# One decoder block on one core: two side chains that step at the ends of units, a transpose with a unit of its own, zeros in four parts

## The chip, the core and the metric

The kernel runs on one core of one Trainium2 chip. The metric is the device time of one execution, in microseconds (us). TensorE (PE) multiplies, VectorE (DVE), ScalarE (ACT) and GpSimd (POOL) work element by element, and SyncE (SP) issues most DMAs. Each engine takes its own instructions in the order in which the program wrote them.

## The reference

One layer of a hybrid decoder on x of 4096 tokens by 1024 features, all in float32:

- h = rms_norm(x), times one matrix w_in, whose columns feed two groups of four heads each.
- Group A, gated delta net: a short convolution and SiLU on q, k and v; normalised q and k; per chunk a triangular solve; a state S that is carried from chunk to chunk; a gated norm.
- Group B, retention: rotary phase on q and k; attention inside a chunk with a fixed decay; a state carried from chunk to chunk; a norm, gated by a SiLU gate.
- x = x + [o_a, o_b] w_out. Then a router picks one of 8 groups of experts and two of its 8 experts for each token; each expert is a SwiGLU of 1024 to 256 to 1024; their weighted sum is added to x, and a last norm closes the block.

## The kernel before, in words

**Stages.** The tokens are worked in 8 super-blocks of 512, counted from 0. Each has four stages of some 60 us, in the order (a,1), (b,1), (a,0), (b,0): the letter is the head group, the digit the pair of heads. After the eighth super-block come the output projection and the router, and from about 2568 us on the experts.

**Units.** A stage is a row of units: the projection of one tile (`proj_n`, `proj_t`: 24 matmuls, lines 231 to 245), which keeps TensorE busy for some 3 us, and behind it a call of `unit`, which does small work in an order that the table `STEPS` gives for each kind of unit. L steps the chains, E evacuates the projection's accumulator, T and B run what is left over, W and S prepare weights. An (a) stage has four g units (gate) and twelve of kinds h and t (q, k, v). A (b) stage has eight r units (q and k: evacuated by VectorE, lines 836 and 839, and summed by POOL), four v units and four y units (gate: line 278). The accumulator `acc` has two buffers: the projection of a unit can't start before the unit two earlier was evacuated.

**Chains.** Two generators make the rest of the head groups, a step at a time. Lane `la` holds the delta-net chain (`gdn_pair`). It starts when an (a) stage ends and runs through the (b) stage behind it and on into the next; a string of digits, `PLAN[pr]`, says how many steps each call of `la.tick` takes. Its steps are: 1 to 3, keys and queries; 4 to 7, the four halves of the attention matrices (TensorE lines 702 and 703, VectorE 708 and 710); 8, the diagonal blocks, which ScalarE copies (line 717, four times) and VectorE transposes in one instruction of 128x1024 (line 718); 9 and 10, v is turned (TensorE 655, VectorE 723 and 726); 11 to 18, a recurrence on VectorE of some 14 us (lines 732 to 738); 19 and 20, transposes back (745, 751); then solves and states. The first eight units of a (b) stage are r units, so steps 1 to 10 fall on them. Lane `lb` holds the retention chain (`ret_pair.chain`): six steps, which transpose a tile of q and k (TensorE 861, 862), multiply (869 to 882), and end with VectorE's 875 and 884 and the output norm. That norm goes from ScalarE's squares to VectorE 287, POOL 288 and back to VectorE 293. The chain starts before the four y units and ends in the g units of the next stage. Before the change `proj_n` steps `lb` in the middle of a projection.

**Zeros.** `zero` clears the table of routed tokens (`tab`) and the output (`out_dram`) from a tile of zeros, `zt`, with one DMA each per super-block, at the start of the first stage (in super-block 0 of the third). The tile has 64 columns, so that its packets have 256 bytes.

**The end of the router part.** `post` steps three generators: `pend` (the top-2 routing of two tiles), `side` (`classes`, the sorting of experts into classes by their counts of the older tokens) and the output projection. `rank` merges the counts and ends the sorting. `warm(n)` issues n transposes of the identity matrix whose results nobody reads (line 1091); the last call comes before the experts, whose first tokens a gather brings in.

Of the kernel before, what the change touches and what calls it, by code (L numbers as in the profile page):

```python
# [8 lines left out]
F32 = mybir.dt.float32  # L9
# [8 lines left out]
P = 128  # L18
D = 1024
KC = D // P  # L20
T = 512
NT = T // P
EPS = 1e-6
ZW = 64
HA = 4
DK = 128
GA, BA = 1536, 2048
# [33 lines left out]
def rows(ap, off, pat):  # L61
    return bass.AP(tensor=ap.tensor, offset=ap.offset + off, ap=pat)
# [6 lines left out]
def mixer(tc, outer, banks, x, attn_norm, w_in, conv_a, a_log, dt_bias, norm_a, norm_b, cst, rope, mixed, clear, w_out, x1, wsp):  # L69


    nc = tc.nc
    S = x.shape[-2]
# [4 lines left out]
    with ExitStack() as ctx:  # L78
# [10 lines left out]
        pcol = cp.tile([P, 48], F32, name="pcol")  # L89
        arow = mp.tile([P, D], F32, name="arow")  # L90
        nrow = cp.tile([P, 128 + 512 + 8], F32, name="nrow")
        nega = cp.tile([P, 4], F32, name="nega")
        dtb = nrow[:, 644:648]
        ex = cp.tile([P, 16], F32, name="ex")
        halo = cp.tile([P, 12, 3], F32, name="halo")
# [56 lines left out]
        def ahead(m, u, kept):  # L152

            if (MS <= m and m + 4 <= M0) != kept:
                return
            if not kept:
                split(m + u)
            elif u == 0:
                for i in range(4):
                    split(m + i)  # L160
# [46 lines left out]
        def unit(u, evac, kind):  # L207

            due = len(stores)
            if u == 3:  # L210
                store()
            g = gi[0]
            act = dict(L=la.tick, E=evac or (lambda: None), T=later, S=lambda: ahead(4 * g + 5, u, False),
                       W=lambda: ahead(4 * g + 5, u, True), B=behind)
            for o in STEPS[kind]:
                act[o]()
            if u == 3:
                gi[0] += 1
            else:
                store(due)  # L220
# [17 lines left out]
        def proj_n(i, n):  # L238
            a = pacc.tile([P, T], F32, name="acc")
            for k in range(KC):  # L240
                wh, wl = w(k)
                s = slice(i * P, i * P + P)
                nc.tensor.matmul(a[:, :n], hh[:, k, s], wh[:, :n], start=(k == 0), stop=False)  # L243
                nc.tensor.matmul(a[:, :n], hh[:, k, s], wl[:, :n], start=False, stop=False)  # L244
                nc.tensor.matmul(a[:, :n], hl[:, k, s], wh[:, :n], start=False, stop=(k == KC - 1))  # L245
                if k == KC // 2 - 1:
                    lb.tick()
            return a

        def take(a, ch, o, ready):  # L250
# [143 lines left out]
        with tc.manual_schedule():  # L394
# [42 lines left out]
            for sb in range(NS):  # L437
                t0 = sb * T
                last = sb == NS - 1
                rt = mp.tile([P, NT, 192], F32, name="rt", bufs=1)  # L440
                nc.sync.dma_start(rt, rows(rope, t0 * 192, [[192, P], [P * 192, NT], [1, 192]]))
                for kind, pr in stages:
                    if (kind, pr) == (("a", 1) if sb else ("a", 0)):
                        for t in clear:
                            zero(nc, t, zt, sb, NS)
                    if kind == "a":

                        n = 264 if pr else 256
                        gs = []
                        if pr:  # L450
                            ba = gp.tile([P, NT, 8], F32, name="ba")
                        for i in range(NT):
                            if pr and not sb:
                                setup(i)
                            if pr and sb and i == 2:
                                next_rows(4 * sb + 3)
                            a = proj_n(i, n)

                            def evac():
                                if pr:  # L460
                                    nc.vector.tensor_copy(ba[:, i], a[:, 256:264])
                                gs.append(silu_gate(a, nrow[:, None, :128].to_broadcast([P, 2, P]), 2))
                            unit(i, evac, "g")
                        if pr:
                            dec = decays(ba)
                            co = next(dec)
                            bg += [lambda: next(dec)] + [lambda: None] * 1 + [lambda: next(dec), lambda: box.append(next(dec))]
                            box = []


                        dst, ready = [], []
                        for wi in range(3):
                            dst.append(gp.tile([P, 2, T], F32, name="qkv"[wi] + "t", bufs=(1, 2, 1)[wi]))
                            for cc in range(2):
                                if wi == 2 and cc == 0:
                                    first = preload(pr, box[0])
                                ch = wi * 4 + 2 * pr + cc
                                a = proj_t(cc)
                                unit(2 * cc + 1, lambda: take(a, ch, dst[wi][:, cc], ready), "t")
                        la.start(gdn_pair(tc, sb, pr, co, first, gs, dst, ready, L), PLAN[pr])  # L480
                    else:
                        if last and pr and sb:
                            out.begin()
                        if pr == 0:
                            for r in range(min(NXI, NT)):
                                bg += x_prep(4 * sb + 4 + r)

                        def after(i):
                            next_rows(4 * sb + 4 + i)
                            if last and i < 0:  # L490
                                mid.close()
                                out.pool = pool(tc, outer, "mt", 2)
                            if last and sb and i == 1:
                                out.turn(0)

                        ret_pair(tc, sb, pr, rt, unit, L, after if pr == 0 else None)
# [124 lines left out]

STEPS = dict(g="WLTBES", h="WLBST", t="WELSTB", r="WEBLTS", v="WSBLET", y="WLETSB")

PLAN = ['12122113121120011111111111111111', '12122012212111111111111111111111']
BETA, GC, NEGC, EGC, DEC, ELAST, TMP = range(7)
NWR, NWH, NXI, NCV = 4, 9, 3, 2


def zero(nc, t, zt, i, n):

    m = int(np.prod(t.shape)) // (n * P * ZW)
    nc.sync.dma_start(rows(t, i * m * P * ZW, [[m * ZW, P], [ZW, m], [1, ZW]]),
                      zt[:, None, :].to_broadcast([P, m, ZW]))


def gdn_pair(tc, sb, pr, co, first, gs, qkv, ready, L):
# [369 lines left out]
def post(tc, out, wrg, wre, sh, tab, then):  # L1006
# [3 lines left out]
    with ExitStack() as ctx:  # L1010
# [13 lines left out]
        with tc.manual_schedule():  # L1024
# [48 lines left out]
            def on(gens):  # L1073
                try:
                    return next(gens[0])
                except StopIteration:
                    gens.pop(0)
# [9 lines left out]
            def warm(n):  # L1087

                t = out.ptr.tile([P, 4, P], F32, name="tr")
                for i in range(n):  # L1090
                    nc.tensor.transpose(t[:, i % 4], sh.ident, sh.ident)

            def turn_x(end):
                r = turned[0]
                if r >= end:
                    return
                turned[0] += 1
                i, sb = r % NT, r // NT
                if i == 0:
                    rst[sb] = [sp.tile([P, NT], F32, name=n) for n in ("ssq", "rst")]  # L1100
                    xT[0] = Split(ap.tile([P, KC, T], F32R, name="xh", bufs=1), ap.tile([P, KC, T], F32R, name="xl", bufs=1))
                if r < back[1]:
                    xi = again.pop(r)
                else:
                    xi = out.xi.pop(r)
                out.split_t(xi, xT[0].hi, xT[0].lo, slice(i * P, i * P + P))
                jx = ap.tile([P, D], BF, name="jx", bufs=1)
                nc.scalar.activation(jx, xi, AF.Square, accum_out=rst[sb][0][:, i:i + 1])
                reload(end)

                n = 2 if sb == NR // NT - 1 else NT
                if (i + 1) % n == 0:

                    while pend and not (on(pend) and r == NR - 1):
                        pass
                    sl = slice(i + 1 - n, i + 1)
                    part = Split(*(t[:, :, sl.start * P:sl.stop * P] for t in (xT[0].hi, xT[0].lo)))
                    new = (route(tc, (r + 1 - n) * P, n, out.x.shape[-2], sh, (rst[sb][0][:, sl], rst[sb][1][:, sl]), part,
                                      wr, usb, oneb, oacc, oaf, tab, scat, (out.pacc, out.ptr, out.psm, sp)))
                    next(new)  # L1120
                    while pend:
                        on(pend)
                    pend.append(new)
                    if sb == NR // NT - 2:
                        older[0] = new
                        side.append(classes(tc, sh, oneb, oacc, out.psm, sp))
# [25 lines left out]
            while pend:  # L1152
                on(pend)
            rank(tc, sh, oneb, oacc, out.psm, sp, warm)
            warm(110)


def route(tc, t0, n, S, sh, rst, xT, wr, usb, oneb, oacc, oaf, tab, scat, pools):
# [671 lines left out]
```

## Time and profile before

| what | value |
|---|---|
| median of 3 runs (lowest to highest) | 3522.51 us (3521.28 to 3523.02) |
| the profiled execution, its time | 3520.8 us |
| its span | 3518.8 us |
| mean granted TensorE clock | 0.991 of full speed |
| TensorE busy | 3391.6 us, 96% of the span, 24347 matmuls |
| VectorE / ScalarE / GpSimd busy | 2166.2 us (62%) / 1502.5 (43%) / 1009.8 (29%) |
| DMA | 463375 packets, 710.98 MB; 151329 packets under 512 B |

The span lies 2.0 us below the execution's own time, and that time 1.7 us below the median. TensorE is busy nearly always, so the time is TensorE's work, what it waits, and the stretches in which its clock is granted at half.

### The profile page before, as it was taken

What the parts mean: (1) busy time and instruction counts of PE and PEld (TensorE: products, weight loads), DVE (VectorE), ACT (ScalarE), POOL (GpSimd) and SP (SyncE); (2) the same over time, 40 slices, a digit from 0 to 9 for tenths busy, and PEclk for the clock granted to TensorE, in tenths of its full rate; (3) what the DMA queues carried; (4) which work ended last, traced back from release to release, by engine and by line L of the source; (5) the groups of instructions that cost most, each with busy time, mean ns of one, the idle gap of its engine ahead of it and who ended that gap; (6) DMA issues with size and microseconds to landing.
All of it is one profiled execution on the core that took longest, in us unless ns stands there. A gap on an engine that the chain in (4) does not pass through costs nothing. (4 is left out here: it accounts for less than half of the span.)

```text
span 3518.8 us, 65226 instructions
## 1 busy us (share of the span) xinstructions
PE 3391.6 (96%) x24347; PEld 3107.5 (88%) x24347; DVE 2166.2 (62%) x5718; ACT 1502.5 (43%) x3322; POOL 1009.8 (29%) x1320
## 2 busy tenths in 40 slices
PE   7999999999999999999999999999999999999996
PEld 6989999999999999999899998888888888888885
DVE  6685575576466466566655644444556676777775
ACT  4344233233333333333332322222246667766775
POOL 1222222232232222222222211111124444444553
PEclk9999999999999999999999999999999999999998
DMA  8776446356455464464464444333368898999995
GB/s 274 208 241 210 149 150 215 131 170 204 158 161 200 141 192 159 162 194 160 159 192 163 143 134 161 115 109 109 113 218 280 290 313 295 310 327 327 331 324 189
DMA packets 463375, 710.98 MB, mean 202 GB/s; under 512 B 151329, under 2 KB 342481, under 8 KB 463057
## 3 DMA queue, kind: packets, MB, share of 16 engines
q1 hardware_dynamic: 426688, 622.03, 53.7%
q0 software_dynamic: 34976, 84.20, 6.8%
q8 instruction: 193, 3.16, 0.4%
q14 instruction: 126, 1.02, 0.1%
q10 hardware_dynamic: 1392, 0.56, 0.1%
HBM read 606.19 MB, written 131.99 MB: 210 GB/s over the span
## 5 line engine op out<-in xcount | busy, mean ns | idle before, releaser
L243 PE MATMUL acc<-wq,hh 128*128 128x256 f32 (+1 forms) x2560 | 750.2, 293 | 38.6 <-DVE rb L839 24.3
L245 PE MATMUL acc<-wq,hl 128*128 128x256 f32 (+1 forms) x2560 | 723.1, 282 | 2.1 <-DVE hl L323 2.1
L244 PE MATMUL acc<-wq,hh 128*128 128x256 f32 (+1 forms) x2560 | 723.6, 283 | 0.2 <-DVE wq L145 0.2
L243 PEld LDWEIGHTS acc<-wq,hh 128*128 128x128 f32 x2560 | 486.5, 190 | 49.2 <-issue 28.1
L245 PEld LDWEIGHTS acc<-wq,hl 128*128 128x128 f32 x2560 | 484.9, 189 | 2.8 <-DVE hl L323 2.8
L244 PEld LDWEIGHTS acc<-wq,hh 128*128 128x128 f32 x2560 | 486.5, 190 | 0.6 <-DVE wq L145 0.5
L231 PE MATMUL acc<-hh,wq 128*128 128x512 f32 x768 | 317.6, 414 | 0.0
L233 PE MATMUL acc<-hh,wq 128*128 128x512 f32 x768 | 302.0, 393 | 0.0
L232 PE MATMUL acc<-hl,wq 128*128 128x512 f32 x768 | 300.9, 392 | 0.0
L1641 PEld LDWEIGHTS g<-xT,gu 128*128 128x128 f32 x2048 | 273.5, 193 | 12.1 <-DVE xT L1573 2.5
L1641 PE MATMUL g<-xT,gu 128*128 128x128 f32 (+30 forms) x2048 | 278.9, 295 | 0.4 <-DVE xT L1573 0.3
L1641 PE MATMUL u<-xT,gu 128*128 128x128 f32 (+30 forms) x2048 | 276.3, 293 | 0.0
L1641 PEld LDWEIGHTS u<-xT,gu 128*128 128x128 f32 x2048 | 266.7, 191 | 1.9
L271 DVE SCALAR_TENSOR_TENSOR cv<-xin,pcol,cv 128x512 f32<-128x512 f32 x288 | 216.3, 751 | 73.6 <-ACT cv L269 66.5
L279 POOL TENSOR_TENSOR gs<-gs,nrow 128x256 f32<-128x256 f32 x128 | 97.0, 758 | 541.6 <-DVE gs L278 515.5
L840 POOL TENSOR_TENSOR rqk<-rqk,rb 128x256 f32<-128x256 f32 x128 | 115.9, 906 | 250.2 <-DVE rb L839 178.4
L1616 POOL DMA_INDIRECT out_dram<-xg,mi x100 | 132.8, 1328 | 185.8 <-DVE ss L1612 93.8
L966 PE MATMUL y<-dh,hh 128*128 128x512 f32 (+16 forms) x400 | 164.6, 412 | 22.0 <-ACT ys L1584 15.3
L1584 ACT ACTIVATE ys<-y,mf 128x512 f32<-128x512 f32 (+22 forms) x200 | 133.4, 679 | 113.2 <-PE y L968 98.1
L1587 POOL DMA_INDIRECT xg<-out_dram,mi x97 | 98.4, 1015 | 266.9 <-PE tr L1571 37.1
L233 PEld LDWEIGHTS acc<-hh,wq 128*128 128x128 f32 x768 | 144.2, 188 | 32.9
L288 POOL TENSOR_TENSOR ss<-ss,ex 128x2 f32<-128x2 f32 x128 | 101.8, 795 | 239.9 <-DVE ss L287 206.7
(377 smaller groups left out, 7940.3 us busy)
## 6 DMA issues: line engine op xcount, KB each, us to landing
wq<-wsp SPq DMA_DIRECT2D x420, 512.0 KB
gu<-in_w_gate_dram SPq DMA_DIRECT2D x128, 512.0 KB
gu<-in_w_up_dram SPq DMA_DIRECT2D x128, 512.0 KB
dn<-in_w_down_dram SPq DMA_DIRECT2D x64, 1024.0 KB
xi<-in_x_dram SPq DMA_DIRECT2D x64, 512.0 KB
wsp<-wq SPq DMA_DIRECT2D x60, 512.0 KB
mixed<-mx SPq DMA_DIRECT2D x128, 128.0 KB
out_dram<-zt SPq DMA_DIRECT2D x8, 2048.0 KB
```

What stands on the lines that cost most here:

```text
L231: nc.tensor.matmul(a, wh[:, s], hh[:, k, :], start=(k == 0), stop=False)
L232: nc.tensor.matmul(a, wh[:, s], hl[:, k, :], start=False, stop=False)
L233: nc.tensor.matmul(a, wl[:, s], hh[:, k, :], start=False, stop=(k == KC - 1))
L243: nc.tensor.matmul(a[:, :n], hh[:, k, s], wh[:, :n], start=(k == 0), stop=False)
L244: nc.tensor.matmul(a[:, :n], hh[:, k, s], wl[:, :n], start=False, stop=False)
L245: nc.tensor.matmul(a[:, :n], hl[:, k, s], wh[:, :n], start=False, stop=(k == KC - 1))
L271: nc.vector.scalar_tensor_tensor(cv, xin[:, j:j + T], tap(j), cv, op0=OP.mult, op1=OP.add)
L840: nc.gpsimd.tensor_tensor(o.rearrange("p h s d -> p (h s d)"), o.rearrange("p h s d -> p (h s d)"), b.rearrange("p h s d -> p (h s d)"), o ...
L966: nc.tensor.matmul(out, a.hi, b.hi, start=(i == 0), stop=False)
L1584: nc.scalar.activation(self.y[:R, s], y[:R], AF.Copy, scale=self.f[:R, WT, self.n:self.n + 1])
L1616: so = nc.gpsimd.indirect_dma_start(out=orow, out_offset=self.idx(0), in_=self.xg[:self.G], in_offset=None, bounds_check=S - 1, oob_is_err ...
L1641: nc.tensor.matmul(o[:, b, :R], self.w.gu[k // 4][:, k % 4, i * DE + b * P:i * DE + b * P + P], self.xT[:, k, :R], start=(k == 0), stop=(k ...
```

## The change

1. `lb` no longer steps in the middle of a projection. `unit` steps it, in g and y units, right behind `la`.
2. In both strings of `PLAN` step 8 (line 718) moves from the unit that also makes the last half of the attention matrices to the next one. In (b,0) that one also has step 9, in (b,1) it had none.
3. `zt` has 256 columns instead of 64, and `zero` takes the largest width that divides: 704 bytes for `tab`, 1 KB for `out_dram`. Each super-block's share is cleared in four parts, one at the start of each stage; in super-block 0 in two, at the third and the fourth stage. The whole is 28672 packets, by the shapes, where before it was 99328.
4. `side` is stepped once more, each time that a routing starts, so that `classes` runs a step earlier.
5. The last call of `warm` issues 140 transposes in place of 110.
6. `nega` becomes a part of `nrow`, which makes room for `zt`.

```diff
-ZW = 64
+ZW = 256
...
-        nega = cp.tile([P, 4], F32, name="nega")
+        nega = nrow[:, 640:644]
...
-            act = dict(L=la.tick, E=evac or (lambda: None), T=later, S=lambda: ahead(4 * g + 5, u, False),
+            def chains():
+                la.tick()
+                if kind in "gy":
+                    lb.tick()
+
+            act = dict(L=chains, E=evac or (lambda: None), T=later, S=lambda: ahead(4 * g + 5, u, False),
...
-                if k == KC // 2 - 1:
-                    lb.tick()
             return a
...
-                    if (kind, pr) == (("a", 1) if sb else ("a", 0)):
-                        for t in clear:
-                            zero(nc, t, zt, sb, NS)
+
+                    k = stages.index((kind, pr))
+                    for t in clear:
+                        if sb:
+                            zero(nc, t, zt, 4 * sb + k, 4 * NS)
+                        elif k >= 2:
+                            zero(nc, t, zt, k - 2, 2 * NS)
...
-PLAN = ['12122113121120011111111111111111', '12122012212111111111111111111111']
+PLAN = ['12121213121120011111111111111111', '12121112212111111111111111111111']
...
-    m = int(np.prod(t.shape)) // (n * P * ZW)
-    nc.sync.dma_start(rows(t, i * m * P * ZW, [[m * ZW, P], [ZW, m], [1, ZW]]),
-                      zt[:, None, :].to_broadcast([P, m, ZW]))
+    size = int(np.prod(t.shape)) // (n * P)
+    w = max(w for w in range(1, ZW + 1) if size % w == 0)
+    m = size // w
+    nc.sync.dma_start(rows(t, i * m * P * w, [[m * w, P], [w, m], [1, w]]),
+                      zt[:, None, :w].to_broadcast([P, m, w]))
...
+                    if side:
+                        on(side)
...
-            warm(110)
+            warm(140)
```

Three places show what this does to VectorE's order. The changed kernel's line numbers are higher: line 718 is its 727, 836 and 839 its 845 and 848, 313 its 316, 723 and 726 its 732 and 735.

The first is VectorE in the r units of stage (b,0), super-block 3. `at` and `am` are the last half of the attention matrices, `U<-X` is the transpose of diagonal blocks, `rqk` and `rb` the evacuation of a unit, `xi` the norm of the next super-block's rows. Before:

```order
1260 L708 SCALAR_TENSOR_TENSOR at<-sm,tk,E 128x128 x2
1261 L710 TENSOR_TENSOR am<-sm,E 128x256
1262 L718 STREAM_TRANSPOSE U<-X 128x32x32
1263 L836 TENSOR_TENSOR rqk<-acc,rt 128x256
1264 L839 TENSOR_TENSOR rb<-acc,rt 128x2x64 x2
1265 L313 SCALAR_TENSOR_TENSOR xi<-xi,st,arow 128x1024
1266 L723 TENSOR_SCALAR tk<-tk 128x8
1267 L726 TENSOR_TENSOR vr<-tr,tk 128x512
1268 L836 TENSOR_TENSOR rqk<-acc,rt 128x256
```

And in the changed kernel:

```order
1260 L717 SCALAR_TENSOR_TENSOR at<-sm,tk,E 128x128 x2
1261 L719 TENSOR_TENSOR am<-sm,E 128x256
1262 L845 TENSOR_TENSOR rqk<-acc,rt 128x256
1263 L848 TENSOR_TENSOR rb<-acc,rt 128x2x64 x2
1264 L316 SCALAR_TENSOR_TENSOR xi<-xi,st,arow 128x1024
1265 L727 STREAM_TRANSPOSE U<-X 128x32x32
1266 L732 TENSOR_SCALAR tk<-tk 128x8
1267 L735 TENSOR_TENSOR vr<-tr,tk 128x512
1268 L845 TENSOR_TENSOR rqk<-acc,rt 128x256
```

The transpose stood ahead of the evacuation of the next unit and now stands behind it, and behind the norm of the rows. In (b,1) it moves behind an evacuation in the same way, and there no norm stands between.

The second is VectorE in the y units of stage (b,1), super-block 3: `gs` is the evacuation of a unit, `X<-V` and `U<-X` are steps 19 and 20 of the delta-net chain, `ram`, `Sb`, `ss` and `mx` are of the retention chain. Before:

```order
1176 L278 SCALAR_TENSOR_TENSOR gs<-th,acc 128x256
1177 L884 TENSOR_TENSOR ram<-sm,cst 128x256
1178 L745 STREAM_TRANSPOSE X<-V 32x32x8 x4
1179 L278 SCALAR_TENSOR_TENSOR gs<-th,acc 128x256
1180 L875 TENSOR_TENSOR Sb<-sm,Sb 128x256
1181 L884 TENSOR_TENSOR ram<-sm,cst 128x256
1182 L287 SCALAR_TENSOR_TENSOR ss<-ss,cst 128x2
1183 L293 SCALAR_TENSOR_TENSOR mx<-sm,ss,gs 128x128 x2
1184 L751 STREAM_TRANSPOSE U<-X 128x512 x2
1185 L278 SCALAR_TENSOR_TENSOR gs<-th,acc 128x256
```

And in the changed kernel:

```order
1176 L281 SCALAR_TENSOR_TENSOR gs<-th,acc 128x256
1177 L754 STREAM_TRANSPOSE X<-V 32x32x8 x4
1178 L893 TENSOR_TENSOR ram<-sm,cst 128x256
1179 L281 SCALAR_TENSOR_TENSOR gs<-th,acc 128x256
1180 L760 STREAM_TRANSPOSE U<-X 128x512 x2
1181 L884 TENSOR_TENSOR Sb<-sm,Sb 128x256
1182 L893 TENSOR_TENSOR ram<-sm,cst 128x256
1183 L290 SCALAR_TENSOR_TENSOR ss<-ss,cst 128x2
1184 L296 SCALAR_TENSOR_TENSOR mx<-sm,ss,gs 128x128 x2
1185 L281 SCALAR_TENSOR_TENSOR gs<-th,acc 128x256
```

A step of the delta-net chain came behind the retention step of the same unit and now comes ahead of it; each unit's evacuation follows both, as before.

The third is VectorE at the end of the router part: `OH` and `ob` are of the last routing, `jk` and `q` of `classes`, `oh` is what TensorE's line 1356 (line 1367 of the changed kernel) takes from `rank`, and `xi` with `acc` evacuates a half of the output projection. Before:

```order
3247 L1247 RECIPROCAL r_29119<-r_29119 128x2
3248 L1249 TENSOR_TENSOR ob<-OH_29135,OH_29141 128x128
3249 L1304 SCALAR_TENSOR_TENSOR jk_24636<-cr,q,cst_24627 64x64
3250 L1305 SCALAR_TENSOR_TENSOR jk_24636<-cr,q,jk_24636 64x64
3251 L1306 SCALAR_TENSOR_TENSOR jk_24636,q<-jk_24636,same 64x64
3252 L1307 SCALAR_TENSOR_TENSOR jk_24636,q<-cst_24627,q,pl 64x32
3253 L576 TENSOR_TENSOR xi_28578<-acc,xi_28578 128x512
3254 L1349 TENSOR_SCALAR q<-q 64x1
3255 L1350 TENSOR_SCALAR q<-q 64x1
3256 L1351 TENSOR_TENSOR q<-q 64x1
3257 L1353 TENSOR_SCALAR oh<-cst_24627,q 64x64
```

And in the changed kernel:

```order
3251 L1258 RECIPROCAL r_29166<-r_29166 128x2
3252 L1260 TENSOR_TENSOR ob<-OH_29182,OH_29188 128x128
3253 L1360 TENSOR_SCALAR q<-q 64x1
3254 L1361 TENSOR_SCALAR q<-q 64x1
3255 L1362 TENSOR_TENSOR q<-q 64x1
3256 L1364 TENSOR_SCALAR oh<-cst_24670,q 64x64
3257 L583 TENSOR_TENSOR xi_28621<-acc,xi_28621 128x512
3258 L1369 CAST pe<-sm 1x4
```

The four rows of `jk` are gone from this place (they stand earlier, ahead of a row `xl`), and the evacuation moved behind `oh`.

## Rows read from the trace of the kernel before

**Rows 1.** TensorE waits, whole run: waiting tile, line, releaser; us, times, longest.

```profile
PE acc L243 <- DVE rb L839: 24.3, 17, 2.3
...
PE acc L243 <- DVE gs L278: 6.0, 8, 2.3
...
PE tr L1571 <- ACT xg L1564: 4.8, 1, 4.8
...
PE tr L547 <- DMA xi<-mixed: 3.3, 1, 3.3
PE sm L1356 <- DVE oh L1353: 2.8, 1, 2.8
PE sm L791 <- DVE Sa L813: 2.6, 1, 2.6
```

**Rows 2.** VectorE timeline, super-block 4, (b,1): start, us, line, operands, idle and releaser.

```profile
1120.74 2.18 DVE L718 STREAM_TRANSPOSE U<-X 128x1024 f32<-128x1024 f32 x1 [1.43 <-ACT X L717]
...
1123.05 0.55 DVE L839 TENSOR_TENSOR rb<-acc,rt 128x128 f32<-128x128 f32 x2
```

**Rows 3.** TensorE timeline: the same place, then (b,0) of super-block 3.

```profile
1121.81 0.60 PE L655 MATMUL tr<-id,vt 128*128 128x128 f32 x4
1123.74 0.36 PE L243 MATMUL acc<-wq,hh 128*128 128x256 f32 x1 [1.34 <-DVE rb L839]
...
996.70 0.36 PE L243 MATMUL acc<-wq,hh 128*128 128x256 f32 x1 [1.62 <-DVE rb L839]
...
1019.34 0.38 PE L243 MATMUL acc<-wq,hh 128*128 128x256 f32 x1 [0.31 <-DVE gs L278]
```

**Rows 4.** VectorE timeline, super-block 3, (b,0).

```profile
991.91 0.41 DVE L710 TENSOR_TENSOR am<-sm,E 128x256 f32<-128x256 f32 x1
993.75 2.13 DVE L718 STREAM_TRANSPOSE U<-X 128x1024 f32<-128x1024 f32 x1 [1.43 <-ACT X L717]
995.75 0.41 DVE L836 TENSOR_TENSOR rqk<-acc,rt 128x256 f32<-128x256 f32 x1
996.05 0.50 DVE L839 TENSOR_TENSOR rb<-acc,rt 128x128 f32<-128x128 f32 x2
996.45 1.30 DVE L313 SCALAR_TENSOR_TENSOR xi<-xi,st,arow 128x1024 f32<-128x1024 f32 x1
...
1000.59 1.51 DVE L732 SCALAR_TENSOR_TENSOR V<-U,V 128x31 f32<-128x31 f32 x4
```

**Rows 5.** VectorE waits of line 293 (output norm), all 128 pairs.

```profile
  POOL ss L288: 101.8, 65
```

**Rows 6.** Windows: start:end, us, busy us (instructions) per engine, granted clock, DMA share, GB/s.

```profile
108.00:111.60 3.60, 3.60 (x20) 3.60 (x19) 1.56 (x4) 0.58 (x1) 0.80 (x2) 0.53 0.88 305
147.00:166.00 19.00, 19.00 (x162) 17.67 (x161) 8.23 (x17) 6.17 (x16) 6.34 (x9) 1.00 0.98 222
2531.60:2538.40 6.80, 6.75 (x33) 6.27 (x34) 4.02 (x24) 2.23 (x4) 0.00 (x0) 0.50 0.52 186
2568.00:2579.40 11.40, 11.34 (x56) 11.11 (x57) 6.01 (x40) 2.19 (x2) 5.91 (x6) 0.50 0.65 160
```

**Rows 7.** Timelines of SyncE, ScalarE and TensorE, super-block 0, (a,0).

```profile
147.18 6.83 SPq L632 DMA_DIRECT2D out_dram<-zt  x1
...
169.42 0.63 ACT L144 ACTIVATE wq<-wr 128x512 fp32r<-128x512 f32 x1 [7.77 <-DMA mixed<-mx]
...
177.92 0.75 PE L791 MATMUL sm<-Sa,kt 128*128 128x128 f32 x4 [2.59 <-DVE Sa L813]
```

**Rows 8.** Timelines of VectorE and TensorE, end of the router part.

```profile
2530.43 0.68 DVE L576 TENSOR_TENSOR xi<-acc,xi 128x512 f32<-128x512 f32 x1
...
2531.64 0.69 PE L1356 MATMUL sm<-oh,cst 64*128 64x64 f32 x2 [2.78 <-DVE oh L1353]
```

**Rows 9.** TensorE timeline, from the router part into the experts.

```profile
2550.90 12.23 PE L1091 MATMUL tr<-cst 128*128 128x128 f32 x110
2567.96 1.28 PE L1571 MATMUL tr<-cst,xg 76*128 76x76 f32 x8 [4.83 <-ACT xg L1564]
```

## The prediction

> **What bounds the kernel now.** I read the page's busy times first: TensorE is busy 96% of the span, so only its own work, its waits and its clock can give time. Then the waits by engine [rows 1]: the largest that this change can reach are 24.3 us in 17 waits for `rb`, the evacuation of a unit in the r units, and 6.0 us in 8 for `gs`; behind them three single waits of 2.6, 2.8 and 4.8 us. Only one wait is for a DMA (3.3 us, a load of `mixed` after the last super-block, which nothing here touches). Then the timelines at those places, and last the windows of granted clock [rows 6].
>
> Split by time, the 17 waits are: eight in (b,1), one in each super-block, 2.20 us in super-block 0 and 1.25 to 1.34 in the seven others, 11.2 in sum; seven in (b,0), 2.28 in super-block 0 and six of 1.56 to 1.62, 11.8 in sum; and two short ones in super-block 0, 1.4. All fifteen long ones look alike. VectorE reaches the transpose of line 718, waits 1.43 us for ScalarE's four copies, spends 2.13 to 2.18 us on it, and only then evacuates a unit that TensorE had long finished [rows 2, 4]; TensorE has no free accumulator meanwhile [rows 3].
>
> **Line 718 in (b,1).** The unit that stands behind the transpose was finished before VectorE idled: TensorE had projected yet another and turned v at 1121.81 [rows 3]. So the evacuation now fits into the 1.43 us of idling: the two lines took 0.45 and 0.55 [rows 2]. It ends at about 1120.1 where TensorE wants it at 1122.4 (1121.81 + 0.60). The wait goes whole: **11.2 us**. Late next is the following evacuation: the transpose starts perhaps at 1120.7 as before and ends at 1122.9, the evacuation at 1123.7, and TensorE needs that one only after its next projection, some 3 us after 1122.4. VectorE then idles again, so the delay of the chain (nothing, or some 0.1 us) is lost in it.
>
> **Line 718 in (b,0).** Here VectorE itself is the limit: its rows follow each other with no gap from the attention matrices to the recurrence, but for the one idle of 1.43 us [rows 4]. What goes in front now is the evacuation and the norm: from 992.25 to 993.05, then to 994.25 (1.3 us with its overlap) [rows 4]. The transpose finds its copies ready (they were at 993.75), so the idle is gone and all that follows is 1.4 us earlier: the recurrence starts at 999.2 in place of 1000.59. TensorE has no wait where it had 1.62, but some 0.2 a unit later, since the second evacuation still stands behind the transpose. The 0.31 us before the second y unit stays [rows 3], because it is VectorE that is late there too. Super-block 7 has no norm there and waits for other lines of the same queue; I count it like the rest. So this gives 1.43 for each of seven super-blocks, 10.0, and in super-block 0, where VectorE has weights to split besides, I take 1.0: **11.0 us**, less than the sum of the waits.
>
> **The half clock in super-block 0.** After the wait of 2.20 us (line 243, 107.0) the clock was granted at 0.53 for 3.6 us [rows 6], 1.2 GHz in place of 2.4. Without the wait those matmuls take half: **1.7 us** (at most 1.8).
>
> **The retention chain at the ends of units.** No instruction is added. TensorE does the same matmuls with the same number of borders of work in its queue or fewer; I cost them at nothing. Their cover is the second accumulator: in a y unit the evacuation `gs` stands on VectorE behind `mx`, which waits for POOL's `ss`, 101.8 us in 65 waits, 1.57 each [rows 5]. With the retention matmuls half a unit later, `gs` comes about 3 us after the projection's end, later than before by one or two, and is needed when the next projection has ended. I count **0**; the bounds are a gain of the small remaining `gs` waits outside super-block 0 (3.7 of the 6.0 [rows 1]) and a loss that is the third rival.
>
> **Zeros.** In (a,0) of super-block 0 SyncE issues the output's share for 6.83 us [rows 7]; while its packets run (147 to 166) the DMA engines are busy 0.98 of the time at only 222 GB/s [rows 6]. ScalarE waits 7.77 us there for the weights of line 144, VectorE behind it, and at last TensorE 2.59 [rows 7]. With half of the bytes at this place, in packets of 704 and 1024 bytes, the weights come at least 7 us earlier, more than the whole wait: **2.6 us**. In the later super-blocks TensorE waits for no DMA [rows 1], so there it gives nothing.
>
> The Trainium skill (DMA: Bandwidth & Descriptors, Specifications) puts the smallest transfer at full rate at 512 bytes and a DMA engine at some 27 GiB/s. By that the 3.2 MB of a whole share would take an estimated 7 us, where the row's 222 GB/s make it 14; the trace bears it out so far as its 256-byte packets move 222 GB/s. By the rule or by the row alone this term is the same 2.6, since halving suffices.
>
> **`classes` a step earlier.** TensorE waits 2.78 us for `oh` [rows 8], while VectorE is busy without a pause. Ahead of `oh` no longer stand one evacuation (0.68 us [rows 8], 0.6 with overlap) and two copies of some 0.1 each: 0.8 us, the wait becomes 2.0. The counts themselves (four rows `jk`) only move up in the same busy stretch. Behind the wait the clock was 0.50 for 6.8 us [rows 6], with 6.75 of them busy, so at most 3.4 more if it stays full; part of that stretch waits for VectorE, so 2.3. Whether it stays I can't read: single waits of 1.62 [rows 3] and even 2.59 [rows 7] were followed by full clock, one of 2.20 by half. The term is 0.8 or 3.1; I take the middle, **2.0 us**.
>
> **`warm(140)`.** The 110 transposes took 12.23 us, 0.111 each, and ended at 2563.1; the first turn of gathered tokens starts at 2567.96, 4.83 later, released by ScalarE [rows 9]. Thirty more take 3.3 us and end at 2566.5, still before the tokens, so they delay nothing and leave 1.5 us idle. After the wait of 4.83 the clock was 0.50 up to 2579.4 with 11.34 us busy [rows 6]; at full clock that is 5.7 less. After 1.5 us the clock should stay full, as after the seven waits of about 1.6 us. A little will be lost to the copies between turns and matmuls: **5.0 us**, with 0 and 5.7 as ends. In the experts TensorE waits for no DMA [rows 1], so the gain carries to the end.
>
> `nega` in `nrow` is set up once and costs nothing; the wider `zt` is cleared long before it is read.
>
> **Sum.** 11.2 + 11.0 + 1.7 + 0 + 2.6 + 2.0 + 5.0 = 33.5 us, from the profiled 3520.8 to 3487.3. That execution lies 1.7 below the median of 3522.5, so the runs should come to 3489. Its own range is 3475 (3.7 of `gs`, 1.1 of `classes`, 0.7 of `warm`, the end of other short waits in super-block 0, and of half clocks after them) to 3496.
>
> **The rivals.**
> - *The clock stays low* (0.2). After 2.0 and after 1.5 us of idling it falls all the same. Then `warm` gives 0 and `classes` 0.8: 33.5 - 5.0 - 1.2 = 27.3, so 3495; if the half clock of super-block 0 stays too, 3497. For it: half clock after 2.20. Against it: full clock after 1.62, seven times, and after 2.59.
> - *The stall only moves* (0.12). VectorE is the limit in both (b) stages, the 1.43 us idle reopens before another row, and the next evacuation waits as long as this one did. Then the 22.2 us of line 718 go, and 11.3 remain: 3511. For it: what I found in (b,0), where a wait and a later one trade places. Against it: in (b,1) VectorE idles after the next evacuations.
> - *Slower* (0.08). Both chains at one border put `mx` with its wait of 1.57 us, and the matmuls of two steps, ahead of each `gs`. If `gs` comes later than the next projection's end, TensorE waits in every unit that steps both, six in each of 16 stages. A wait of 0.35 us in each of these 96 eats the whole sum; from 0.42 on (40.3 us) the kernel is slower by more than 0.2%; at 0.45 it comes to 3522.5 - 33.5 + 43.2 = 3532. For it: VectorE is late already at the second y unit in (b,0) [rows 3]. Against it: by the rows there are about 3 us of slack elsewhere.
> - *The zeros collide at another place* (0.04). In super-block 0 the second half now falls on (b,0), whose weights are also loaded there in halves; 2.6 us come back, 3492. A part of it may hit (a,1) of later ones, where TensorE waited for no DMA.
> - *Nothing* (0.06). The same mechanism at a smaller price, 0.3 us in each of the 96 units, costs 28.8 and leaves 4.7: 3518.
>
> **How the numbers follow.** The forecast has 0.5. I predict 3489. The range goes from 3475, its own low end, to 3510, which takes in the clock, the zeros and most of the moved stall and leaves out the slower case and the null. What a measurement of this kernel can tell from no change is 0.2%, 7 us. Faster than 3515.5 are the forecast, the first two rivals and the fourth, 0.86, less 0.04 for an unseen cost: 0.82. Within: 0.10. Slower: 0.08.
>
> **What would show it.** In the profile after, the waits of line 243 for `rb` fall from 24.3 to under 4 us; VectorE's 718 (727 then) has no idle ahead of it in (b,0) and keeps some 0.7 in (b,1). `gs` waits stay at 6 or less; a sum over 15 there, or new waits of the retention matmuls, is the third rival. The window behind `warm` shows a clock of 1.00 with an idle of 1.5 us ahead, or the first rival. The wait for `Sa` (2.6) is gone. I am wrong if VectorE's recurrence in (b,0) doesn't start earlier against TensorE's units, or if line 243 waits at a new place as often as before.

## The result and the profile after

The changed kernel takes 3484.75 us, median of 4 runs (3481.66 to 3486.27), where the kernel before takes 3522.02 beside it: ratio 0.9895, 95% interval 0.9883 to 0.9907, 37 us less. The profiled execution took 3483.95 us with a span of 3482.0, 36.8 less than the span before.

TensorE's waits over the whole run, as in [rows 1]:

```profile
PE acc L248 <- DVE gs L281: 6.8, 8, 2.9
...
PE tr L554 <- DMA xi<-mixed: 3.3, 1, 3.3
PE acc L248 <- DVE rb L848: 2.8, 3, 1.4
...
PE sm L1367 <- DVE oh L1364: 2.3, 1, 2.3
...
PE sm L772 <- DVE Sb L884: 1.9, 1, 1.9
...
PE tr L1582 <- ACT xg L1575: 0.9, 1, 0.9
```

The waits for `rb` fell from 24.3 us in 17 to 2.8 in 3. Those for `gs` are 6.8 where they were 6.0, the wait for `Sa` is gone, and the one for `Sb` ahead of line 772 is 1.9 us.

The timeline of VectorE in (b,1), super-block 4, as in [rows 2]:

```profile
1101.73 0.41 DVE L719 TENSOR_TENSOR am<-sm,E 128x256 f32<-128x256 f32 x1
1102.06 0.42 DVE L845 TENSOR_TENSOR rqk<-acc,rt 128x256 f32<-128x256 f32 x1
1102.39 0.48 DVE L848 TENSOR_TENSOR rb<-acc,rt 128x128 f32<-128x128 f32 x2
1103.57 2.21 DVE L727 STREAM_TRANSPOSE U<-X 128x1024 f32<-128x1024 f32 x1 [0.70 <-ACT X L726]
```

And that of TensorE at the same place, as in [rows 3]:

```profile
1104.39 0.29 PE L249 MATMUL acc<-wq,hh 128*128 128x256 f32 x1
1104.52 0.28 PE L250 MATMUL acc<-wq,hl 128*128 128x256 f32 x1
1104.64 0.60 PE L664 MATMUL tr<-id,vt 128*128 128x128 f32 x4
1104.99 0.36 PE L248 MATMUL acc<-wq,hh 128*128 128x256 f32 x1
```

The evacuation (845, 848) now stands ahead of the transpose (727), whose idle is down from 1.43 to 0.70 us. TensorE goes from the turns of v (664) straight into the next projection, 0.35 us after their start. Before it was 1.93 us (1121.81 to 1123.74): the step of 1.58 us is 0.24 more than the idle of 1.34 that the waits counted, because line 248 starts 0.25 us before the record of 664 ends (1104.64 + 0.60), where after a wait it starts behind that end.

VectorE in (b,0), super-block 3, as in [rows 4]:

```profile
976.27 0.42 DVE L719 TENSOR_TENSOR am<-sm,E 128x256 f32<-128x256 f32 x1
976.60 0.42 DVE L845 TENSOR_TENSOR rqk<-acc,rt 128x256 f32<-128x256 f32 x1
976.93 0.48 DVE L848 TENSOR_TENSOR rb<-acc,rt 128x128 f32<-128x128 f32 x2
977.33 1.28 DVE L316 SCALAR_TENSOR_TENSOR xi<-xi,st,arow 128x1024 f32<-128x1024 f32 x1
978.52 2.21 DVE L727 STREAM_TRANSPOSE U<-X 128x1024 f32<-128x1024 f32 x1
...
983.52 1.24 DVE L741 SCALAR_TENSOR_TENSOR V<-U,V 128x31 f32<-128x31 f32 x3
```

No idle is left ahead of the transpose. The norm (316) fills it, as reckoned, and the recurrence starts 7.25 us after the last `am`, where it was 8.68 (991.91 to 1000.59): 1.43 us.

To see where the 36.8 us lie, I took the start of each stage's first projection from the two timelines and compared the stages' lengths. The experts' first large tile is their first matmul of 128x256:

| stretch | shorter by, us |
|---|---|
| start and (a,1) of super-block 0 | -3.0 |
| (b,1) of super-block 0 | 3.6 |
| (a,0) of super-block 0 | 2.9 |
| (b,0) of super-block 0 | 3.1 |
| (b,1) of super-blocks 1 to 7 | 11.3 (1.57 to 1.67 each) |
| (b,0) of super-blocks 1 to 6 | 10.9 (1.42, 1.43, and four of 1.95 to 2.15) |
| (a) stages of super-blocks 1 to 7 | 0.3 |
| (b,0) of super-block 7, and on to the wait for `oh` | 0.5 |
| from there to the first tokens of the experts | 1.8 |
| from there to the experts' first large tile | 5.1 |
| the rest | 0.3 |

The first row is no part of the change: in the traces of the experiments that have the kernel before's own code there, that stretch is 2 to 3 us longer too. The execution that was profiled before had drawn a short half clock at its start: 6.8 us in its first 50 us, where the other traces have 10.2 to 17.

### The profile page after: what moved, and what is told of

It is laid out like the page before. It is cut to its first block, busy times and chain, and to the rows that moved or that the text cites. A ratio compares the mean times of both kernels' runs of the same rounds, so it can differ in the third digit from the quotient of the medians.

```text
span 3482.0 us, 65321 instructions
## 1 busy us (share of the span) xinstructions
PE 3382.3 (97%) x24377; PEld 3102.6 (89%) x24377; DVE 2160.8 (62%) x5718; ACT 1492.9 (43%) x3322; POOL 1010.6 (29%) x1320
## 5 line engine op out<-in xcount | busy, mean ns | idle before, releaser
L975 PE MATMUL y<-dh,hh 128*128 128x512 f32 (+16 forms) x400 | 164.5, 411 | 21.7 <-ACT ys L1595 13.9
```

Of the source, the lines that this page charges most:

```text
L975: nc.tensor.matmul(out, a.hi, b.hi, start=(i == 0), stop=False)
```

## The experiments

Each had 4 to 11 runs beside 15 to 27 of the kernel before, which alone scattered from 3514.7 to 3530.8 us. So an interval is about 3 to 6 us to either side.

**The strings of PLAN alone**, on the kernel before.

```diff
-PLAN = ['12122113121120011111111111111111', '12122012212111111111111111111111']
+PLAN = ['12121213121120011111111111111111', '12121112212111111111111111111111']
```

> The kernel before with the two strings of PLAN alone (the transpose of diagonal blocks a unit later). My theory: each (b,1) loses its wait for rb and each (b,0) the 1.43 us idle of VectorE, whatever else is done; the trace of the changed kernel shows 1.6 us for a (b,1) and 1.4 to 2.1 for a (b,0) in super-blocks 1 to 7, so about 22 us there and 4 more in super-block 0: 3496 us, ratio 0.9925, and these numbers by stage. Rival: the stages' gain comes from the chains at the ends of units as well: then at most two thirds of it here, 3505 or more, ratio 0.995 or above, and the rest in the run of the chains alone.

3496.86 us, ratio 0.9925 (0.9911 to 0.9938). By stages: (b,1) 3.6 us in super-block 0 and 10.6 in the other seven, (b,0) 1.6 and, in super-blocks 1 to 6, 10.6. The waits:

```profile
PE acc L243 <- DVE gs L278: 6.9, 8, 3.1
...
PE acc L243 <- DVE rb L839: 2.7, 3, 1.4
```

The (b,1) stages of super-blocks 1 to 7 and the (b,0) stages of 1 to 6 gain here all but 0.1 us each of what they gain in the whole change, so the transpose's place is shown as the cause, and the rival, that the chains give a third of it, falls.

**The chains at the ends of units alone.**

```diff
-            act = dict(L=la.tick, E=evac or (lambda: None), T=later, S=lambda: ahead(4 * g + 5, u, False),
+            act = dict(L=chains, E=evac or (lambda: None), T=later, S=lambda: ahead(4 * g + 5, u, False),
...
-                if k == KC // 2 - 1:
-                    lb.tick()
```

> The kernel before with the retention chain stepped at the ends of g and y units alone. My theory: the same matmuls, hidden evacuations, nothing gained: 3522 us, ratio 0.999 to 1.001, and no (b) stage changes by over 0.2 us; after the last super-block one wait for Sb grows by 1 us. Rival 1: fewer breaks in the row of projections give 0.09 us each at some 96 places, 8 us: ratio 0.998 or less. Rival 2 (the slower case): evacuations come late, waits for gs grow by 0.3 us and more in each unit: ratio 1.005 or more.

3523.38 us, ratio 1.0001 (0.9992 to 1.001). The (b,1) stages are 0.06 us shorter each, the (b,0) the same, but for one of -0.49 (its line 726, which is 723 before, lasted 0.72 us; more on that below).

```profile
PE acc L248 <- DVE gs L281: 6.7, 8, 2.9
...
PE sm L766 <- DVE Sb L878: 1.9, 1, 1.9
```

The waits for `gs` are 6.7 us, of 6.0 before, and the kernels that keep the chains in the middle have 5.7 to 7.0: the second accumulator hides the later evacuations, as far as these sums can tell. The wait for `Sb` after the last super-block is 1.9 us where it was 0.9, as in the changed kernel. Fewer breaks gain nothing, and the slower case doesn't come.

**The changed kernel with the chains in the middle again** (the same edit backwards).

> The changed kernel with the retention chain stepped in the middle of projections, as before. My theory: the chains' place is worth nothing with the rest either, or the 0.1 us for each (b,1) by which the changed kernel beats the strings of PLAN alone, some 1 us: 3485 to 3486 us, ratio 0.9895 to 0.990. Rival: together with the new PLAN it is worth the 0.3 us of more in each (b) stage: 3489, ratio 0.991.

3486.54 us, ratio 0.9906 (0.9892 to 0.992): the same as the changed kernel within the intervals. Its (b,1) stages gain 10.9 us in place of 11.3, its wait for `Sb` is 0.9.

**The zeros alone** (the edits 3 and 6 of the change).

```diff
-                    if (kind, pr) == (("a", 1) if sb else ("a", 0)):
-                        for t in clear:
-                            zero(nc, t, zt, sb, NS)
+                    k = stages.index((kind, pr))
+                    for t in clear:
+                        if sb:
+                            zero(nc, t, zt, 4 * sb + k, 4 * NS)
+                        elif k >= 2:
+                            zero(nc, t, zt, k - 2, 2 * NS)
```

> The kernel before with the zeros alone (four parts, wider packets, and nega in nrow). My theory: only the third stage of super-block 0 gains, the 2.6 to 2.9 us of its wait: 3519 us, ratio 0.9992. Rival: smaller and shorter bursts free the loads elsewhere too; the parts measured so far (strings of PLAN 25, chains 0, warm 0, classes 1 to 3) leave some 9 us of the 37 of the whole change, and all of them come from here: 3513, ratio 0.9975.

3517.26 us, ratio 0.999 (0.9981 to 0.9999). The third stage of super-block 0 is 2.85 us shorter, later ones are the same within 0.6, but for (b,0) of super-block 0: it is 1.0 shorter, with one stretch of half clock in place of two. In the changed kernel the timeline of SyncE has, as in [rows 7]:

```profile
147.06 0.77 SPq L641 DMA_DIRECT2D out_dram<-zt  x1
```

And that of ScalarE:

```profile
160.40 1.14 ACT L144 ACTIVATE wq<-wr 128x512 fp32r<-128x512 f32 x2
```

The issue takes 0.77 us in place of 6.83, for half of the bytes, and the instruction of line 144 that waited 7.77 us until 169.42 is now the second of these two, right behind the first. Whether the halves or the wider packets did it wasn't run apart. The rival's 9 us are not here.

**The earlier steps of `classes` alone.**

```diff
                     pend.append(new)
+                    if side:
+                        on(side)
```

> The kernel before with the earlier steps of classes alone. My theory: the wait for oh falls from 2.78 to 2.3 us and the half clock behind it is half as long, as in the trace of the changed kernel; the sorting ends 1 to 2 us earlier, and the first gather of the experts comes earlier by as much: 3520.5 us, ratio 0.9995, at the edge of what can be told. Rival: the half clock's length belongs to chance, not to the wait: the window is as long as before, and nothing but 0.5 us is gained.

3521.73 us, ratio 0.9992 (0.9983 to 1.0001). The wait for `oh` is 2.2 us where it was 2.8:

```profile
PE sm L1358 <- DVE oh L1355: 2.2, 1, 2.2
```

Behind it this execution kept full clock; ahead of the experts it had half clock for 20.5 us.

**The changed kernel without them.**

> The changed kernel with classes stepped as before. My theory: the wait for oh is 0.5 us longer and the half clock behind it, 3.4 us in the changed kernel, 6.8 again: 2 us slower, 3487 us, ratio 0.990. Rival: the length of that half clock is chance, nothing changes: 3485, ratio 0.9895.

3491.75 us, ratio 0.9916 (0.9903 to 0.993), and the wait for `oh` is 3.1 us:

```profile
PE sm L1365 <- DVE oh L1362: 3.1, 1, 3.1
```

The half clock behind this longer wait lasted 3.4 us, no longer than behind the 2.3 us of the changed kernel; so its length doesn't go with the wait, as the rival had it. The 7 us of difference are more than that mechanism can give (2 us expected). The profiled execution was the slowest of the five, 16.7 us longer than the changed kernel's. Of these, 1.5 lie in (b,0) of super-block 0 and some 3 behind the last projection of super-block 7, both with half clocks that the other trace doesn't have; 10.2 lie behind the first tokens of the experts, and only 0.4 between `oh` and those tokens. So most of what this execution lost lies where the edit changes nothing; where the 7 us of the medians come from isn't shown.

**140 transposes alone.**

```diff
-            warm(110)
+            warm(140)
```

> The kernel before with 140 in place of 110 transposes ahead of the experts, alone. My theory: the idle ahead of the first turn falls from 4.83 to 1.5 us, the clock stays at 1.00 behind it, and the experts start their first large matmuls 5 us earlier: 3517 us, ratio 0.9985. Rival: the clock falls all the same, or the gain is lost further on to loads of the experts' weights: ratio 0.9995 to 1.0005.

3525.17 us, ratio 1.0005 (0.9995 to 1.0015). In this trace the idle ahead of the first turn (line 1571) is 1.21 us and the clock full behind it, but some 9 us later TensorE begins to wait, three times, for nothing that the profile shows, and between the second wait and the third the clock falls. From its waits:

```profile
PE u L1641 <- issue: 2.3, 3, 1.1
...
PE tr L1571 <- ACT xg L1564: 1.2, 1, 1.2
```

And two windows of it, with the granted clock behind POOL's busy time:

```profile
2568.00:2578.40 10.40, 8.64 (x77) 8.47 (x78) 6.97 (x41) 3.77 (x5) 5.75 (x6) 1.00 0.63 161
2578.40:2585.20 6.80, 5.89 (x20) 4.99 (x20) 4.50 (x7) 3.04 (x3) 0.15 (x1) 0.50 0.99 244
```

**The same kernel again.**

> The kernel of the run of 140 transposes alone once more, unchanged. There the trace had three waits of TensorE, 2.3 us, for nothing that the profile shows, right after the start of the experts, a half clock behind them, and the time was that of the kernel before. Theory A, the waits come with this code: they stand in this trace again, ratio 1.000. Theory B, chance of one execution: they are gone, and the 4 to 6 us that 140 are worth in the changed kernel show, 3517 us, ratio 0.9985.

3521.67 us, ratio 1.0003 (0.9994 to 1.0012). The hidden waits are gone, but theory B's gain doesn't come either: the clock fell all the same, for 10.2 us, behind an idle of 1.40. The wait of this execution:

```profile
PE tr L1571 <- ACT xg L1564: 1.4, 1, 1.4
```

And the window behind it:

```profile
2569.00:2580.90 11.90, 11.10 (x58) 10.95 (x58) 6.20 (x40) 2.77 (x4) 5.93 (x6) 0.57 0.70 186
```

**148 on the kernel before.**

> The kernel before with 148 transposes, which by the row of 140 end 0.3 us ahead of the tokens. If the gain of warm hangs on the idle ahead of the first turn, this gains as much as 140 do in the changed kernel or more: 3516 us, ratio 0.9985 or less. If the added instructions themselves cost as much as the clock gives when the rest of the kernel is the old one, it stays at 1.000.

3522.07 us, ratio 1.0001 (0.9992 to 1.001): nothing gained, with an idle of 0.47 us. The clock was full behind the first turn, and the hidden waits are there again, with half clock behind them:

```profile
PE u L1641 <- issue: 2.3, 4, 1.1
```

**The changed kernel with 110, 125 and 155** (the same line with other numbers).

> The changed kernel with 110 transposes ahead of the experts in place of 140. My theory: in the changed kernel the trace shows full clock behind the 140, so without them the half clock comes back and the kernel is 5 us slower: 3490 us, ratio to the kernel before 0.991. Rival, from the run of warm alone: the clock won there is given back in the experts, by waits of all engines for their own instructions, and on the whole it is worth nothing: 3485 us, ratio 0.9895.

> The changed kernel with 125 transposes. The idle ahead of the first turn is then about 2.6 us, between the 0.9 of 140 and the 4.2 of 110. Theory of the clock: the half clock comes back in some executions, the time lies between those of 110 and 140. Rival: idle time there costs nothing either way, the three are the same within 2 us.

> The changed kernel with 155 transposes, which end about 0.8 us after the tokens are there, so that TensorE has no idle ahead of the first turn. Theory of the idle: the half clock, which one of two kernels with 140 still showed, is gone for good, and the kernel is up to 1 us faster than the changed one: 3484 us, ratio 0.989. Rival: the half clock behind the first turns comes of the narrow matmuls and short waits that follow, not of the idle: 3486 us or slower.

They take 3490.97 us (0.9913, 0.99 to 0.9927), 3487.46 (0.9901, 0.9883 to 0.9918) and 3491.39 (0.9915, 0.9902 to 0.9929). The changed kernel, with 140, lies below all of them, but each interval reaches into its own (0.9883 to 0.9907). A window of the changed kernel behind the first turn:

```profile
2536.00:2547.00 11.00, 9.85 (x89) 9.46 (x89) 8.25 (x44) 4.81 (x6) 5.62 (x6) 1.00 0.64 171
```

The same of the one with the chains in the middle, also with 140:

```profile
2535.20:2544.20 9.00, 8.68 (x50) 8.53 (x51) 6.95 (x42) 3.27 (x4) 4.09 (x5) 0.62 0.55 144
```

And two of the one with 155:

```profile
2539.00:2550.70 11.70, 9.20 (x83) 9.04 (x82) 7.00 (x42) 3.65 (x5) 5.93 (x6) 1.00 0.65 162
2550.70:2554.10 3.40, 3.40 (x13) 2.89 (x13) 2.58 (x4) 2.92 (x3) 0.00 (x0) 0.50 0.95 243
```

With the same 140 and the same idle (0.91 and 0.92 us), one execution kept the clock and the other lost it. Without any idle it was lost 11.5 us later, and there too behind waits for nothing that the profile shows:

```profile
PE u L1652 <- issue: 2.1, 2, 1.1
```

So these waits aren't the chance of one execution. Four traces had full clock up to these matmuls of `u`, those of 140 alone, of 148, of 155 and of the changed kernel, and the first three waited there; of the ten that had lost the clock by then, none did. What is waited for isn't shown. From the first turn to the experts' first large tile the traces give 14.8 to 18.5 us with 110 (six of them), 17.8 with 125, and 10.5, 13.7, 13.9, 15.4 and 15.4 with 140 in five traces, 14.1 with 148, 13.5 with 155. So 140 save some 2 us in the mean there, and 1.7 one tile further on, where the half clock of the run of 140 alone is counted too. The 5.1 of the changed kernel's own profile are the best case, and the idle alone doesn't decide.

## Why the prediction was right, and where its sizes were off

Forecast 33.5 us, measured 37; the time is 4 us below the forecast and inside the forecast's own range. Of that range's low end the terms with a price carry 5.5 us, to 3483.5; the rest, to 3475, has none.

- **Line 718 in (b,1): right, too small.** The waits vanished in all eight. A wait cost more than the idle the view shows, since TensorE's records overlap where it doesn't wait, and this overlap is lost at each stop: 10.6 us in super-blocks 1 to 7 with the strings of PLAN alone, 0.23 each above the bare waits that I had summed, 9.0, and 0.24 at the place shown above. The whole change gives another 0.1 each; 0.06 of it comes with the chains, by both runs of them.
- **Line 718 in (b,0): right, and a second gain overlooked.** Two of six gain 1.42 and 1.43, to the digit what VectorE's idle was. The other four gain 0.5 more. In these VectorE's line 723 took 0.70 to 0.72 us before; it is a scale of 128x8 that elsewhere takes some 0.2. The whole line before (shortest, median and longest in ns):

```profile
L723 DVE TENSOR_SCALAR tk<-tk x16: 149/212/717, 108.1 to 1999.3; 128x8 f32<-128x8 f32 x16
```

And after, as line 732:

```profile
L732 DVE TENSOR_SCALAR tk<-tk x16: 123/166/193, 109.8 to 1969.5; 128x8 f32<-128x8 f32 x16
```

With the old strings of PLAN such a long one came in two to five of a trace's (b,0) stages, at changing super-blocks, 26 times in seven traces, and with the new strings in none. The traces show what it ended with. A long one and the sum of POOL beside it, in super-block 5:

```profile
1499.23 0.71 DVE L723 TENSOR_SCALAR tk<-tk 128x8 f32<-128x8 f32 x1
...
1498.20 1.72 POOL L840 TENSOR_TENSOR rqk<-rqk,rb 128x256 f32<-128x256 f32 x1 [3.83 <-DVE rb L839]
```

And a short one, in super-block 3:

```profile
997.64 0.19 DVE L723 TENSOR_SCALAR tk<-tk 128x8 f32<-128x8 f32 x1
...
996.63 1.80 POOL L840 TENSOR_TENSOR rqk<-rqk,rb 128x256 f32<-128x256 f32 x1 [3.90 <-DVE rb L839]
```

Each of the 26 ended 0.02 to 0.03 us after that sum did, while the short ones ended in the middle of it. In the new order no instruction of POOL runs beside the line. So the move also took it out from beside POOL's sum; that the sum held it is what these ends suggest, and why it did so in some passes and not in others isn't shown.

In super-block 7, which I had counted with 1.43, the units of the stage end 1.1 us earlier with the strings of PLAN alone; up to `oh` the changed kernel keeps 0.5, with 6.8 us of half clock on the way where there were 3.4. In super-block 0, counted with 1.0, the traces with the new strings give 1.6 to 3.3: there half clocks come and go.
- **The half clock of super-block 0: right.** It came in all seven traces with the old strings of PLAN and in none of the seven with the new ones; (b,1) there gained 3.5 to 3.6 us, wait and clock, of 3.9 forecast.
- **The chains: 0, right.** Two runs, one each way, agree on 0.06 us for a (b,1) and nothing that the times can tell. Only the wait for `Sb` behind the last super-block is 1 us longer, which I hadn't named.
- **Zeros: 2.6 forecast, 2.85 to 2.9 by the stage, 3.5 by the runs.** Right.
- **`classes`: 2.0 forecast.** The wait for `oh` fell by 0.5, not by 0.8; by the runs alone it is worth 0 to 6. The length of the half clock behind `oh` (0 to 6.8 us in the traces) goes with no wait that I could find: 6.8 behind 2.26 and 2.78, 3.4 behind 3.08 and 3.21.
- **`warm`: 5.0 forecast, mis-sized.** The step that failed is "after 1.5 us the clock should stay full". It rested on seven waits of about 1.6 us; there were six, and the seventh in (b,0), 2.28 us in super-block 0, stood beside half clock (237.8 to 241.2), and a wait of 2.29 for `gs` was followed by it too (265.1). Three runs alone gave nothing: the clock fell behind 1.40 and 0.92 us of idle, and where it stayed, three of four traces lost it 10 to 12 us after the first turn, among waits that the forecast didn't have. In the changed kernel the 6 us more against 110 are at the edge of the intervals, and 155, without any idle, are no faster than 110. The profile after shows the forecast's 5 us, by luck of its execution.

So (b,1) and (b,0) gave more than forecast, `warm` less, and they nearly cancel; that the total came so close is in part luck. The parts measured alone add up to 26.4 + 3.5 + 2.8 - 0.4, and some -1 of `warm`: 31 us, with some 8 us of uncertainty, against 37 of 33 to 41 for the whole. Whether the remaining 6 are chance, or a gain that the parts have only together, stays open: the changed kernel's five near relatives took 3486.5 to 3491.8 us.

## What to carry to other kernels

Where an engine waits for another's evacuation, look at what stands ahead of it in that engine's queue: an instruction that itself waits for a third engine may stand one evacuation later, so that the evacuation fills the idle that it would have spent waiting. Count each such stop of TensorE as its idle plus the lost overlap, here 0.23 us. Don't book gains of a clock's state from one profile: two executions of nearly the same code differ there by as much as the gain.

## What the runs showed of the hardware

- The clock: half clock came behind an idle of 0.92 us in one trace, and full clock stayed behind 0.91 in another; in both the engine had run 140 transposes before. Full clock also stayed behind 2.59 in the kernel before [rows 7], amid the projections. The half clock after 140 transposes lasted 0 to 10.2 us in the five traces, and with 110 from 10.2 to 20.5.
- The Trainium skill (TensorE: Matmul & The Clock Gate, Part 1: The HAM clock gate) says that the monitor of the clock runs free and doesn't reset when a kernel starts, so that the point of transition varies. The two executions of one kernel do differ in that point: the half clock began 1.2 us after the first turn started in one (2570.7) and 10.3 us after it in the other (2578.4), there amid the hidden waits. Whether the monitor's running free is the reason, and what it looks at, no run here shows.
- The same kernel scattered by 16 us (27 runs from 3514.7 to 3530.8). Among the places that differ in the traces are half clocks at the start, in (b,0) of super-block 0, behind the wait for `oh` and at the start of the experts.
- A stop of TensorE ahead of matmuls of 128x256 cost 0.24 us beside its idle at the place shown, and 0.23 in the mean of seven.
- A short instruction of VectorE (line 723) that ran beside POOL's sum of 128x256 ended 0.02 to 0.03 us after that sum in 26 of 49 passes, those of (b,0) in super-blocks 0 to 6 of the seven traces with the old strings, and took some 0.5 us more than in the others.
